# Weight sums of the couples: from GpSimd arithmetic to accumulating transfers, and result stores issued half a unit later

## The chip, the cores and the metric

The kernel runs on one core of one Trainium2 chip, as one program. The time is the device time of one execution in microseconds; the number that counts is the median of several executions. Engine names as in the profile: PE is TensorE, PEld its weight loads, DVE is VectorE, ACT is ScalarE, POOL is GpSimd, SP is SyncE. Three of them also issue transfers: SP, ACT and POOL.

## The reference, cut to what matters

The reference is one layer of a hybrid decoder over a prompt of 2048 tokens of width 1024, plus 8 single-token samples, all in float32:

```python
hn = rmsnorm(x) * (1 + scale) + shift
xa, za, q, k, v, glr, zg = split(hn @ w_in)        # widths 1024, 1024, 512, 512, 1024, 16, 1024
xc = conv4(xa); gx, ga = sigmoid(block_diag(xc))   # RG-LRU group
log_a = 8 * ga * log_sigmoid(lru_lambda); a = exp(log_a)
u = sqrt(1 - exp(2 * log_a)) * gx * xc
h_t = a_t * h_{t-1} + u_t
y_lru = h * silu(za)
o = gated_linear_attention(q, k, v, glr)           # 4 heads, per-head RMSNorm
y_gla = o * silu(zg)
x = x + gate * (concat(y_lru, y_gla) @ w_out); y = rmsnorm(x) * g_final
```

The change concerns the columns xa, za and zg of the input projection, and the products with SiLU that follow them.

## The kernel before, in words

The prompt is worked off in two halves of 1024 tokens (TH). In each half the four GLA heads come first (`gla_head`), then the *couples*: pairs of 128-column blocks of `w_in`. `Lru(half, j)` couples columns XA+128j and ZA+128j; `Zg(half, h)` couples the two blocks of zg of one head. A half has eleven couples. The output projection (class `Pair`) follows after the second half.

A couple is a product of weights (1024 by 256) with activations (1024 by 1024), each seen as a 2 by 2 matrix of blocks. It is computed with a scheme of Strassen's kind (Winograd's form): seven block products instead of eight. The right-hand operands are A11, A12, A21, A22 and four combinations S1 to S4, made once per half and kept in SBUF; the weights are B11, B12, B21, B22 and the combinations T1 to T4. Every operand is held as a high part (fp32r) and a low rest, so one product is 4 x 3 matmuls of 128 x 512, into PSUM (`Couple.product`, line 1558). Between products, sums of PSUM banks are made on DVE and ACT (lines 1562 to 1573), and the four results of a couple go to `block`, which applies the convolution and gates (Lru) or the SiLU and the product with the attention output (Zg), and stores them with `spill` (line 712) into the DRAM tensor `mixd`. In the first half the couples' stores are issued by ACT's queue, in the second half by POOL's.

In the first half the weights come raw: `load_raw` fetches 1 MB into one of two buffers, and `prepare(q)` splits one operand with `split`: ACT copies the high part (line 1504), DVE subtracts it for the low part (line 1505), and SP stores both for the second half (line 1507). The combinations are made inside the raw buffer: after B11 is split, `combine` overwrites b11 with T1, makes T2 in a tile `t2`, and overwrites b12 with T3 (lines 1538 to 1540), and after T1 is split, b11 becomes T4 (line 1522). POOL makes these sums, except for the first couple, where DVE makes three of them. `combine` also runs small TensorE products for the samples (line 304, `sample_cols`), which read the raw weights before they are overwritten; their result leaves through the copy in line 305 and the products in line 310. In the second half the split operands are simply read back (`src`).

The order of work is written by hand: `couples` lists the uses of the operands, interleaving two neighbouring couples, and calls `prepare` five uses ahead (`lead=5`). Each use advances a clock by half a unit (`tick(0.5)`), and `after(units, f)` emits `f` when the clock has got that far. Within an engine, instructions run in the order that the framework's scheduler gives them; `behind(q)` ties an emission to the last instruction of queue q.

Of the kernel before, what the change touches and what calls it, by code (L numbers as in the profile page):

```python
# [53 lines left out]
def hybrid_kernel(ctx, tc, i, o):  # L54
# [654 lines left out]
    def spill(y, ct, half, c0, q=S):  # L709

        t0 = (half * TH + c0) // P
        q.dma_start(mixd[t0:t0 + 4, :, ct].rearrange("t p c -> p t c"), y.rearrange("p (t c) -> p t c", c=P))

    def behind(q):

        return tc.issue_after(next(x for x in reversed(list(nc.cur_bb.bb.instructions)) if x.engine == q.engine))
# [403 lines left out]

    def silu(z, src):
        log_exp[0] = False
        S.activation(z, src, AF.Tanh, scale=0.5)
        V.scalar_tensor_tensor(z, z, 1.0, src, op0=OP.add, op1=OP.mult)

# [187 lines left out]
    def second_rows(sc, ready, then):  # L1313
# [22 lines left out]
        def step(p, x, k):  # L1336
            if p == 0 and not ready:
                after(0.5, lambda: step(p, x, k))
                return
            pt = turn(x, (k, k + 4))  # L1340
            f = sc.tile([P, 4, P], F32, tag="f", bufs=2)
            for m in range(2):
                S.activation(f[:, 2 * m:2 * m + 2], pt[:, m * 256:(m + 1) * 256].rearrange("p (j t) -> p j t", j=2),
                             AF.Identity, scale=Gm[:, k + 4 * m, 8:9], bias=Sh[:, k + 4 * m, 8:9])
            G.dma_start(fd[0:4, :, k, p * P:(p + 1) * P].rearrange("o p c -> p o c"), f)
            b = sc.tile([P, 4, P], F32, tag="s", bufs=2)
            G.tensor_tensor(b[:, 0], f[:, 1], f[:, 3], op=OP.add)
            G.tensor_tensor(b[:, 1], b[:, 0], f[:, 0], op=OP.subtract)
            G.tensor_tensor(b[:, 2], f[:, 0], f[:, 1], op=OP.subtract)
            G.tensor_tensor(b[:, 3], f[:, 2], b[:, 1], op=OP.subtract)  # L1350
            G.dma_start(fd[4:8, :, k, p * P:(p + 1) * P].rearrange("o p c -> p o c"), b)
            if k < 3:
                after(1 if k == 1 else 0.5, lambda: step(p, x, k + 1))
            elif p < 3:
                load(p + 1)
            else:
                after(1.5, then)
# [6 lines left out]
    def sums(pool, then):  # L1364
# [8 lines left out]
        def one(k):  # L1373
            s1, s2 = two()
            (h11, l11), (h21, l21), (h22, l22) = [high_low(op, k) for op in (A11, A21, A22)]
            with behind(V):
                add(s1, h21, h22)
                add(s1, s1, l21)

            def more():  # L1380
                with behind(V):
                    add(s1, s1, l22)
                    add(s2, s1, h11, OP.subtract)
                    add(s2, s2, l11, OP.subtract)
                after(0.5, high)
# [15 lines left out]
        def other(k, s2, low):  # L1401
            s3, s4 = two()
            (h11, l11), (h21, l21), (h12, l12) = [high_low(op, k) for op in (A11, A21, A12)]
            with behind(V):
                add(s4, h12, s2, OP.subtract)
                add(s4, s4, l12)

# [56 lines left out]
    class Couple:  # L1464
# [30 lines left out]
        def prepare(self, q, now=False):  # L1495
# [13 lines left out]
            if q == B11:  # L1509
                self.slot(q)  # L1510
                split(q, b11)
                (lambda: self.combine(V)) () if now else after(self.wait, self.combine)
            elif q == T2:
                self.slot(q)
                if now:
                    split(q, self.t2)
                else:
                    after(0.5, lambda: split(q, self.t2))
            elif q == T1:
                self.slot(q)  # L1520
                split(q, b11)
                G.tensor_tensor(b11, b21, self.t2, op=OP.subtract)
            else:
                self.slot(q)
                split(q, {B21: b21, T3: b12, B22: b22, T4: b11}[q])

        def combine(self, q=G):
            r = self.raw
# [8 lines left out]
            t = self.t2 = lp.tile([P, 4, P], F32, tag="t2", name="t2")  # L1537
            q.tensor_tensor(b11, b12, b11, op=OP.subtract)
            q.tensor_tensor(t, b22, b11, op=OP.subtract)
            q.tensor_tensor(b12, b22, b12, op=OP.subtract)  # L1540

# [5 lines left out]
        def product(self, q):  # L1547
# [15 lines left out]
            elif q == 1:  # L1563
                V.tensor_tensor(self.y, self.y, self.p1, op=OP.add)
            elif q == 2:
# [22 lines left out]
    class Zg(Couple):  # L1588
# [34 lines left out]
        def block(self, s, dt, src):  # L1623
            z = self.zs()
            silu(z, src)
            c0 = SEGS[s][0]
            V.tensor_tensor(z, z, self.o[((0, 0), (1, 1), (0, 1), (1, 0)).index((s, dt))], op=OP.mult)
            spill(z, 8 + 2 * self.h + dt, self.half, c0, G if self.half else S)

    smp_lru = {}  # L1630

    class Lru(Couple):
# [18 lines left out]
        def block(self, s, n, src):  # L1651
            if n == 1:
                z = self.zs()
                silu(z, src)
                after(2, lambda: self.out(s, z))
            else:
                self.conv(s, src)
                after((2.5, 2)[s], lambda: self.gates(s))
# [57 lines left out]
        def out(self, s, z):  # L1716
            if not self.res:
                after(0.5, lambda: self.out(s, z))
                return
            c0 = SEGS[s][0]  # L1720
            V.scalar_tensor_tensor(z, self.res[0][:, c0:c0 + 512], 0.5, z, op0=OP.mult, op1=OP.mult)
            spill(z, self.j, self.half, c0, G if self.half else S)

# [761 lines left out]
```

## Time and profile before

| | |
|---|---|
| median of 3 executions | 1461.93 us (1461.71 to 1464.23) |
| profiled execution: its time, its span | 1465.7 us, 1463.9 us |
| PE busy in the span | 1417.0 us (97%) |
| DVE, ACT, POOL busy | 1096.9, 697.1, 205.3 us |
| mean granted TensorE clock | 0.988 |
| first half's couples | about 332 to 600 us |
| second half's couples | about 880 to 1128 us |

The profiled execution is a separate one; its time is 3.8 us above the median. PE's busy time is modelled, since matmuls are pipelined. In rows of instructions the columns are line, engine, operation, output and inputs, count, busy us and mean ns of one, then the engine's idle time just before and what ended it. In rows of waits the engine that waits stands left of the arrow, then total us, number and longest.

### The profile page before, as it was taken

The numbers are of one execution on the slowest core, as the hardware profiler recorded it, in microseconds if no ns is written. First come the engines' busy times: TensorE is split into PE (matmuls) and PEld (weight loads), VectorE is DVE, ScalarE is ACT, GpSimd is POOL, SyncE is SP. The second block draws the span as 40 slices with busy tenths as digits, with TensorE's granted clock in tenths as the row PEclk, the third lists the DMA queues.
The fourth block names the chain that finished last, engine by engine and source line by source line (L and its number), as shares of the span: only waits on it lengthen the run. The fifth ranks groups of instructions, "written<-read, shape, count | busy, mean of one in ns | idle before, by whom it ended". The sixth has DMA issues, their size and how long they took to land.

```text
span 1463.9 us, 22541 instructions
## 1 busy us (share of the span) xinstructions
PE 1417.0 (97%) x8113; PEld 1172.2 (80%) x8113; DVE 1096.9 (75%) x2405; ACT 697.1 (48%) x1310; POOL 205.3 (14%) x255
## 2 busy tenths in 40 slices
PE   8999999999999999999999999998999999999997
PEld 6888989886777777889888888887788787777786
DVE  5767975657888788766776865797966886688886
ACT  4634463635674767334343533766563522144332
POOL 0200154425222212001111100000002000000000
PEclk9999999999999999999999999999999999999999
DMA  9725666648668557965857528888889867684452
GB/s 325 266 88 167 244 229 209 233 134 283 236 242 280 201 195 273 354 218 174 313 170 238 189 87 302 283 278 269 280 258 385 317 228 271 230 339 144 135 173 101
DMA packets 173380, 341.89 MB, mean 234 GB/s; under 512 B 12466, under 2 KB 101842, under 8 KB 169677
## 3 DMA queue, kind: packets, MB, share of 16 engines
q1 hardware_dynamic: 137269, 277.92, 55.7%
q0 software_dynamic: 13392, 46.54, 8.2%
q10 hardware_dynamic: 22608, 15.99, 3.4%
q8 instruction: 64, 1.05, 0.3%
q14 instruction: 47, 0.39, 0.1%
HBM read 205.78 MB, written 134.69 MB: 233 GB/s over the span
## 4 chain that ended last, share of the span: by engine, by line
PE 64%; DVE 12%; DMA 8%; ACT 7%; issue 6%; POOL 1%; SPq 1%; ACTq 0%; DVEq 0%; POOLq 0%
PE acc L2132 11%; PE tp L2132 8%; PE acc L1558 8%; PE tp L1558 7%; PE acc L397 3%; PE acc L396 3%; PE acc L398 3%; PE acc L702 3%; PE acc L704 3%; PE acc L703 3%; DVE cv L1676 2%; DVE tg L1712 2%; PE po L1048 1%; DMA wada<-in_w_ada_dram 1%; DMA op<-fd 1%
## 5 line engine op out<-in xcount | busy, mean ns | idle before, releaser
L1558 PE MATMUL acc<-op,op 128*128 128x512 f32 x1056 | 252.2, 393 | 3.1 <-ACT op L1504 2.8
L1558 PEld LDWEIGHTS acc<-op,op 128*128 128x128 f32 x1056 | 198.5, 189 | 45.9 <-ACT op L1504 3.3
L1558 PE MATMUL tp<-op,op 128*128 128x512 f32 x792 | 201.1, 401 | 2.4 <-DVE acc L1568 2.4
L2132 PE MATMUL acc<-w,a 128*128 128x512 f32 (+1 forms) x792 | 189.3, 392 | 2.8 <-DVE w L1997 2.0
L1558 PEld LDWEIGHTS tp<-op,op 128*128 128x128 f32 x792 | 150.7, 193 | 36.4 <-DVE acc L1568 3.4
L2132 PEld LDWEIGHTS acc<-w,a 128*128 128x128 f32 x792 | 147.9, 189 | 39.8 <-issue 3.4
L396 PE MATMUL acc<-w,op 128*128 128x256 f32 (+1 forms) x508 | 150.4, 296 | 1.5 <-ACT w L374 1.2
L397 PE MATMUL acc<-w,op 128*128 128x256 f32 (+1 forms) x508 | 144.2, 284 | 0.4 <-DVE w L375 0.4
L398 PE MATMUL acc<-w,op 128*128 128x256 f32 (+1 forms) x508 | 144.0, 283 | 0.2 <-DVE op L271 0.2
L2132 PE MATMUL tp<-w,a 128*128 128x512 f32 x564 | 137.2, 393 | 0.0
L2132 PEld LDWEIGHTS tp<-w,a 128*128 128x128 f32 x564 | 105.2, 188 | 27.9 <-issue 5.2
L702 PE MATMUL acc<-op,w 128*128 128x512 f32 x296 | 121.2, 410 | 0.0
L704 PE MATMUL acc<-op,w 128*128 128x512 f32 x296 | 116.7, 394 | 0.0
L703 PE MATMUL acc<-op,w 128*128 128x512 f32 x296 | 115.9, 392 | 0.0
L396 PEld LDWEIGHTS acc<-w,op 128*128 128x128 f32 x508 | 96.2, 190 | 3.3 <-ACT w L374 1.6
L397 PEld LDWEIGHTS acc<-w,op 128*128 128x128 f32 x508 | 95.6, 188 | 1.6 <-DVE w L375 0.6
L398 PEld LDWEIGHTS acc<-w,op 128*128 128x128 f32 x508 | 95.7, 188 | 0.6 <-DVE op L271 0.4
L1994 ACT CAST a<-s 128x512 fp32r<-128x512 f32 x61 | 36.5, 619 | 104.3 <-issue 37.2
L228 ACT ACTIVATE junk<-on 128x256 bf16<-128x256 f32 x64 | 26.8, 418 | 111.3 <-DVE on L1053 98.8
L1676 DVE SCALAR_TENSOR_TENSOR cv<-xa,vecT,cv 128x512 f32<-128x512 f32 x96 | 73.0, 760 | 7.5 <-ACT cv L1674 6.7
L1049 DVE TENSOR_TENSOR states<-states,pkv 128x256 f32<-128x256 f32 x60 | 25.1, 418 | 54.6 <-PE po L1048 54.3
L704 PEld LDWEIGHTS acc<-op,w 128*128 128x128 f32 x296 | 55.6, 188 | 12.5 <-DVE w L375 0.4
(445 smaller groups left out, 2818.8 us busy)
## 6 DMA issues: line engine op xcount, KB each, us to landing
wtd<-op SPq DMA_DIRECT2D x77, 512.0 KB
op<-wtd SPq DMA_DIRECT2D x77, 512.0 KB
w<-parts SPq DMA_DIRECT2D x16, 1024.0 KB
a<-mixd SPq DMA_DIRECT2D x63, 256.0 KB
parts<-w POOLq DMA_DIRECT2D x12, 1024.0 KB, 6.5
w<-wd SPq DMA_DIRECT2D x10, 1024.0 KB
wr<-in_w_in_dram SPq DMA_DIRECT2D x18, 512.0 KB
wada<-in_w_ada_dram SPq DMA_DIRECT2D x16, 512.0 KB
```

Source lines behind the costliest of these rows:

```text
L228: S.activation(junk[:m, :n], x, AF.Square, accum_out=out)
L396: PE.matmul(ps, part(0, kt, c), hi[:, kt % 4], start=kt == 0, stop=False)
L397: PE.matmul(ps, part(0, kt, c), lo[:, kt % 4], start=False, stop=False)
L398: PE.matmul(ps, part(1, kt, c), hi[:, kt % 4], start=False, stop=kt == KT - 1)
L702: PE.matmul(ps[:, :n], hi[:, kt], a, start=kt == 0, stop=False)
L703: PE.matmul(ps[:, :n], hi[:, kt], b, start=False, stop=False)
L704: PE.matmul(ps[:, :n], lo[:, kt], a, start=False, stop=kt == KT - 1)
L1558: PE.matmul(ps, w[:, u, k], t[:, v, k], start=q < 3 and (k, u, v) == (0, 0, 0), stop=(k, u) == (3, 1), skip_group_check=True)
L1676: V.scalar_tensor_tensor(cv, xa[:, k:k + 512], cw[k], cv, op0=OP.mult, op1=OP.add)
L1712: V.tensor_tensor_scan(h, a, tx, 0.0 if self.half == 0 else hc[:, j:j + 1], op0=OP.mult, op1=OP.add)
L1994: S.copy(t[:, 0, k], (low(t) if src is None else src)[:, k])
L2132: PE.matmul(ps, t[:, u, k], w[:, v, k, c], start=(q < 3 or ps is own) and (k, u, v) == (0, 0, 0), stop=(k, u) == (3, 1), skip_group_check= ...
```

## The change

Four things change.

1. Signs. S1, S2, S4 and the corresponding operands of the second half (in `second_rows`) change sign, so that the weights' combinations become plain sums: T1 = b11 + b12, T2 = b22 + T1, T3 = b12 + b22, T4 = b21 + T2. Where a result then comes out negated, `silu` takes -1 for its constant, and one sum of PSUM banks becomes a difference.
2. Place of the sums. For all couples but the first, POOL's four operations go; ACT copies b22 into `t2`, and four transfers issued by POOL with an accumulating operation add in place: b11 += b12, t2 += b11, b12 += b22 and, when B21 has been split, b21 += t2. T4 is then split from b21 instead of b11.
3. T2 is split a whole unit after `prepare` instead of half a unit.
4. `late_spill`: in the first half the couples' stores are emitted half a unit later, behind ACT's last instruction at that time. In the second half nothing changes (POOL).

```diff
+    def late_spill(z, ct, half, c0):
+        def go():
+            with behind(S):
+                spill(z, ct, half, c0)
+        if half:
+            spill(z, ct, half, c0, G)
+        else:
+            after(0.5, go)
...
-    def silu(z, src):
+    def silu(z, src, sign=1.0):
...
-        V.scalar_tensor_tensor(z, z, 1.0, src, op0=OP.add, op1=OP.mult)
+        V.scalar_tensor_tensor(z, z, sign, src, op0=OP.add, op1=OP.mult)
...
             if q == B11:
                 self.slot(q)
                 split(q, b11)
-                (lambda: self.combine(V)) () if now else after(self.wait, self.combine)
+                self.now = now
+                (self.combine if now else lambda: after(self.wait, self.combine))()
...
-                    after(0.5, lambda: split(q, self.t2))
-            elif q == T1:
-                self.slot(q)
-                split(q, b11)
-                G.tensor_tensor(b11, b21, self.t2, op=OP.subtract)
+                    after(1, lambda: split(q, self.t2))
             else:
                 self.slot(q)
-                split(q, {B21: b21, T3: b12, B22: b22, T4: b11}[q])
+                split(q, {T1: b11, B21: b21, T3: b12, B22: b22, T4: b21}[q])
+                if q == B21:
+                    self.add(b21, b21, self.t2)
+
+        def add(self, out, x, y):
+            if self.now:
+                V.tensor_tensor(out, x, y, op=OP.add)
+            else:
+                G.dma_start(out, y, accum_op=OP.add)
...
-            q.tensor_tensor(b11, b12, b11, op=OP.subtract)
-            q.tensor_tensor(t, b22, b11, op=OP.subtract)
-            q.tensor_tensor(b12, b22, b12, op=OP.subtract)
+            if not self.now:
+                S.copy(t, b22)
+            self.add(b11, b11, b12)
+            self.add(t, b22 if self.now else t, b11)
+            self.add(b12, b12, b22)
...
-                V.tensor_tensor(self.y, self.y, self.p1, op=OP.add)
+                V.tensor_tensor(self.y, self.p1, self.y, op=OP.subtract)
...
-            silu(z, src)
+            silu(z, src, -1.0 if dt else 1.0)
...
-            spill(z, 8 + 2 * self.h + dt, self.half, c0, G if self.half else S)
+            late_spill(z, 8 + 2 * self.h + dt, self.half, c0)
...
-            spill(z, self.j, self.half, c0, G if self.half else S)
+            late_spill(z, self.j, self.half, c0)
```

The sums that make S1, S2, S4 (in `sums`) and those in `second_rows` only swap additions and subtractions, one for one.

More of the change, by code (lines that the diff above doesn't have):

```diff
@@ L1346, in step @@
             b = sc.tile([P, 4, P], F32, tag="s", bufs=2)
-            G.tensor_tensor(b[:, 0], f[:, 1], f[:, 3], op=OP.add)
-            G.tensor_tensor(b[:, 1], b[:, 0], f[:, 0], op=OP.subtract)
+            G.tensor_tensor(b[:, 0], f[:, 3], f[:, 1], op=OP.subtract)
+            G.tensor_tensor(b[:, 1], b[:, 0], f[:, 0], op=OP.add)
             G.tensor_tensor(b[:, 2], f[:, 0], f[:, 1], op=OP.subtract)
-            G.tensor_tensor(b[:, 3], f[:, 2], b[:, 1], op=OP.subtract)
+            G.tensor_tensor(b[:, 3], b[:, 1], f[:, 2], op=OP.subtract)
             G.dma_start(fd[4:8, :, k, p * P:(p + 1) * P].rearrange("o p c -> p o c"), b)
@@ L1376, in one @@
             with behind(V):
-                add(s1, h21, h22)
-                add(s1, s1, l21)
+                add(s1, h22, h21, OP.subtract)
+                add(s1, s1, l21, OP.subtract)
             def more():
@@ L1382, in more @@
                     add(s1, s1, l22)
-                    add(s2, s1, h11, OP.subtract)
-                    add(s2, s2, l11, OP.subtract)
+                    add(s2, s1, h11)
+                    add(s2, s2, l11)
                 after(0.5, high)
@@ L1404, in other @@
             with behind(V):
-                add(s4, h12, s2, OP.subtract)
-                add(s4, s4, l12)
+                add(s4, s2, h12, OP.subtract)
+                add(s4, s4, l12, OP.subtract)
             def last():
@@ L1517, in prepare, with combine @@
                 else:
-                    after(0.5, lambda: split(q, self.t2))
-            elif q == T1:
-                self.slot(q)
-                split(q, b11)
-                G.tensor_tensor(b11, b21, self.t2, op=OP.subtract)
+                    after(1, lambda: split(q, self.t2))
             else:
                 self.slot(q)
-                split(q, {B21: b21, T3: b12, B22: b22, T4: b11}[q])
-        def combine(self, q=G):
+                split(q, {T1: b11, B21: b21, T3: b12, B22: b22, T4: b21}[q])
[5 more added lines that the diff above has]
+            else:
+                assert out is x
+                G.dma_start(out, y, accum_op=OP.add)
+        def combine(self):
             r = self.raw
@@ L1653, in block @@
                 z = self.zs()
-                silu(z, src)
+                silu(z, src, -1.0)
                 after(2, lambda: self.out(s, z))
```

## The prediction

> **What bounds the kernel now.** I read the page's head first, then the table of busy time by stage, then, for the one stage that the change works in, the waits of TensorE, and from each of them the timeline backwards.
>
> ```profile
> span 1463.9 us, 22541 instructions
> ...
> PE 1417.0 (97%) x8113; PEld 1172.2 (80%) x8113; DVE 1096.9 (75%) x2405; ACT 697.1 (48%) x1310; POOL 205.3 (14%) x255
> ```
>
> TensorE is busy in 97% of the span, so the whole kernel cannot gain more than what TensorE idles or loses in clock. The couples of the first half, the only place where sums are made from raw weights, lie from about 332 to 600 us (columns: stretch, length, busy us and instructions of PE, weight load, DVE, ACT, POOL, granted clock, DMA share, GB/s):
>
> ```profile
> 332.00:600.00 268.00, 256.14 (x1208) 200.48 (x1209) 222.19 (x321) 175.95 (x274) 71.43 (x50) 0.97 0.71 248
> ```
>
> TensorE idles 11.9 us of 268, and the clock of 0.97 says that it loses some more. DVE is busy 83%, ACT 66%: neither bounds on average, but they fall behind in bursts. Who ends TensorE's idle time there (waited for, us in total, times, longest):
>
> ```profile
> PE acc L310 <- ACT am L305: 3.9, 2, 2.2
> PE acc L1558 <- ACT op L1504: 2.8, 1, 2.8
> PE gps L1693 <- ACT xh L1680: 2.6, 2, 1.7
> PE tp L1558 <- DVE acc L1568: 2.4, 1, 2.4
> PE acc L304 <- DVE tp L1564: 1.2, 1, 1.2
> PE acc L1558 <- DVE zs L1124: 0.3, 1, 0.3
> ```
>
> 13.2 us in seven holes: this list is the purse from which any gain in the stage is paid. The 2.8 us is the start of the stage (the first split), which the change leaves alone.
>
> **Part 1: the sums leave POOL.** For ten couples three POOL sums (L1538 to L1540) and the later difference for T4 (L1522) go; in the first couple DVE does them, with one more add of 0.7 us that T4 needs only six products later (taken at 0, at most 0.7).
>
> ```profile
> L1505 DVE TENSOR_TENSOR op<-raw,op 128x512 fp32r<-128x512 f32 x66 | 54.6, 836 | 5.9 <-ACT op L1504 5.8
> ...
> L1681 DVE TENSOR_TENSOR xl<-cv,xh 128x512 fp32r<-128x512 f32 x16 | 10.9, 684 | 0.1
> ```
>
> The same DVE operation on the same shape takes 684 ns in L1681 and 836 in L1505, the line whose instructions meet POOL's sums: 66 x 0.152 = 10.0 us of DVE time that comes back. A single victim shows the size:
>
> ```profile
> 525.87 1.78 DVE L1505 TENSOR_TENSOR op<-raw,op 128x512 fp32r<-128x512 f32 x1
> ```
>
> 1.78 instead of 0.68 is 1.1 us, and the chain of waits hands it on: the cv operation after it releases ACT's xh, behind which ACT works without a hole through exponential, Tanh, Sqrt and table loads to the gate's product on DVE, and DVE from there through the scan and the next cv to a hole of TensorE twenty us later:
>
> ```profile
> 547.85 0.50 PE L1693 MATMUL gps<-xh,amh 128*128 128x512 f32 x1 [1.66 <-ACT xh L1680]
> ```
>
> So of the two L1693 holes (2.6 us: 1.7 and 0.9) I take 1.1 off the longer and all 0.9 of the shorter: 2.0 us. The hole of 1.2 us behind L1564 goes whole (DVE backlog of the same kind), and half of the 2.4 behind L1568, which ends a DVE queue of scan, products and a split: 1.2.
>
> A shortened hole also saves clock. In the ten us around the hole at 547.85 the granted clock is 0.83:
>
> ```profile
> 545.00:555.00 10.00, 8.34 (x29) 6.13 (x28) 9.96 (x16) 7.19 (x12) 1.63 (x1) 0.83 0.84 265
> ```
>
> That is 1.7 us lost on top of the hole. If the hole falls from 1.66 to 0.6 us, I take that the loss goes with it: 1.7. The Trainium skill ("TensorE: Matmul & The Clock Gate", Part 1: The HAM clock gate) says that the clock is halved after an idle window of about 3.4 us. By that rule a hole of 1.66 us would cost no clock, and my sum would be 1.7 us smaller; the trace does not agree with it as worded, since the clock fell here with no idle of 3.4 us, so I keep the row.
>
> **Part 2: stores wait half a unit.** In the first half each result store sits in ACT's queue directly behind the DVE product it sends out, so ACT stands until DVE is done:
>
> ```profile
> 440.64 0.62 ACT L1504 CAST op<-t 128x512 fp32r<-128x512 f32 x1 [3.42 <-POOL t L1539]
> ...
> 445.73 1.61 ACTq L712 DMA_DIRECT2D mixd<-zs  x3
> ...
> 447.38 0.37 ACT L305 COPY am<-acc 128x256 f32<-128x256 f32 x1 [4.68 <-DVE zs L1627]
> ...
> 447.80 0.30 PEld L310 LDWEIGHTS acc<-sel,am 128*128 128x128 f32 x2 [2.19 <-ACT am L305]
> ```
>
> Read upwards: TensorE waits for the small copy am; that copy waits 4.68 us on ACT behind three stores, which wait for DVE. With the stores emitted half a unit (one product of TensorE) later, the copy passes: of the 3.9 us in two L310 holes this one, 1.7 us, goes, and the 0.3 behind L1124 just before it. The other L310 hole (2.2) stays: no store stands before it. The same store also holds the gate activation of the next segment:
>
> ```profile
> ACT tx L1697 <- DVE tg L1712: 12.4, 5, 3.4
> ...
> ACT tg L1697 <- DVE zs L1721: 6.8, 4, 1.7
> ...
> ACT zs L1123 <- DMA mixd<-zs: 4.1, 1, 4.1
> ```
>
> The 6.8 us of ACT go too, at nothing for TensorE, since its consumer xh hangs on DVE. What is late next: zs has four buffers, and one store's landing already held ACT for 4.1 us; a product later in issue lengthens that one wait. And at the end of the stage the chain runs over a store into the next stage's weights:
>
> ```profile
> 592.80 5.47 DMA mixd<-zs
> 598.29 7.58 DMA w<-parts
> ```
> ```profile
> 605.98 0.19 PEld L396 LDWEIGHTS acc<-w,op 128*128 128x128 f32 x1 [0.42 <-issue]
> ```
>
> The weights land at 605.87, and TensorE's weight load, idle for 0.42 us, follows at once, so nothing covers a later store there: one product, by the following row 2.7 us, is charged in full.
>
> ```profile
> 883.42 2.75 PE acc L1558 x12
> ```
>
> **Part 3: what the accumulating transfers cost.** Added are ten copies of b22 into t on ACT and forty 256 KB transfers issued on POOL, which has no other work in these couples. The copy is like L1504's cast (0.62 us below): 6.2 us of ACT in 268, set against 6.8 us of stores' waits that leave it; 0 on the path. The issue takes 0.75 us of POOL:
>
> ```profile
> L712 POOL DMA_DIRECT2D mixd<-zs x27 | 20.2, 752 | 270.4 <-DVE zs L1721 231.4 <-DVE zs L1627 29.6 <-issue 7.8
> ```
>
> No accumulating transfer is in the trace. The nearest rows are plain POOL transfers of 256 KB, of this stage and of the second half's couples, where DMA is busier (last column: us from issue to landing):
>
> ```profile
> fd<-scratch POOLq DMA_DIRECT2D x3, 256.0 KB, 2.8
> ```
> ```profile
> mixd<-zs POOLq DMA_DIRECT2D x25, 256.0 KB, 5.4
> ```
>
> What hangs on it is T2. Its operand t needs two transfers one after the other, where POOL did two sums:
>
> ```profile
> ACT op L1504 <- POOL t L1539: 15.4, 6, 4.8
> ```
> ```profile
> 460.70 1.28 POOL L1538 TENSOR_TENSOR raw<-raw 128x512 f32<-128x512 f32 x1 [5.65 <-PE acc L304]
> ```
> ```profile
> 463.38 0.62 ACT L1504 CAST op<-t 128x512 fp32r<-128x512 f32 x1 [1.87 <-POOL t L1539]
> ```
>
> Of the ten T2s six hold ACT, 15.4 us in all, 4.8 at most. In the couple shown, before: t is there 2.7 us after POOL starts, ACT arrives at 0.8 and waits 1.9. After: t is there at 2 x (0.75 + 2.8) = 7.1 us or 2 x (0.75 + 5.4) = 12.3, and ACT arrives one product later, at 0.8 + 2.7 = 3.5: a wait of 3.6 or 8.8 us. I take the 2.8 of the same stage: 3.6 us is the size of the present waits on t (3.42 above), and ACT has idle time right after (12.4 us in 5 waits for the scan) that it eats first. TensorE needs T2 five products later. So 0 on the path, and the rival below has the other end. The Trainium skill ("DMA: Bandwidth & Descriptors", Anatomy of one DMA — SWDGE (gpsimd) path) fits such a transfer as 2.0 us plus bytes over 436 GB/s, an estimate of 2.6 us here; by it the wait would be 3.2 and the sum the same. The row of 2.8 agrees with it, the row of 5.4 does not.
>
> Sign changes in T1, S1, S2, S4 and the SiLUs replace one operation by another of the same shape: 0. Where b21 takes its sum, T4 is split five products later: 0. The second half's stores were on POOL and stay.
>
> **Sum.** Holes: 1.7 + 0.3 + 2.0 + 1.2 + 1.2 = 6.4. Clock: 1.7. End of stage: -2.7. Net 5.4 us. The profiled execution (span 1463.9, its time 1465.7) would come to 1460.3; its time lies 3.8 above the median 1461.93, so the median goes to 1456.5. Own range of this case: without clock and with 0.7 for the first couple 1459.0, without the charge at the end 1453.8. A difference under 0.2% (2.9 us) is about what a measurement of this kernel cannot tell from none.
>
> **Rivals.**
>
> A, slower: T2's chain takes over. If a transfer lands after 5.4 us, ACT waits 8.8 us where it waited up to 4.8. In the burst of 437 to 448 us ACT stood 3.4 + 4.7 us and TensorE lost 2.0. At that rate six couples lose 6 x 2.0, three of them clock of 1.7 as well, and the end is charged: 12 + 5.1 + 2.7 = 20 us; the gains of part 1 (about 4 of holes) and part 2 (2.0) still come, so +14: 1476. It decides when a transfer lands after more than about 3.4 us (a wait above 4.8). For it: accumulating reads the destination as well. Against: POOL's queue is free, and TensorE's holes stood beside only one of six present waits on t.
>
> B, slower: DMA becomes the limit.
>
> ```profile
> q10 hardware_dynamic: 13200, 6.56, 8.2%
> ```
>
> This queue (ACT's stores, same 512-byte pieces) uses 8.2% of 268 us, 22 us, for 6.56 MB. Forty times 0.262 MB are 10.5 MB: 35 us, or 70 if the destination's reading costs as much. On 0.71 x 268 = 190 that is 225 to 260 us of 268. At the upper end the present wait on raw weights grows and loads come late in every couple:
>
> ```profile
> ACT op L1504 <- DMA raw<-in_w_in_dram: 3.4, 5, 1.3
> ```
>
> The stage then ends when DMA ends, about 274 us with the first uncovered loads, +6: 1468.
>
> C, hidden: DVE's and ACT's time comes back, but the holes stay where they are, because another operation in the same queues is late; only the end and a hole or two move: 1461.
>
> D, more: all holes but the first go, 10.4 us, with three losses of clock of 1.7, and the end is covered because all of its chain comes earlier: 15.5, so 1446.5.
>
> **How the numbers follow.** Forecast 0.43, A 0.18, B 0.11, C 0.18, D 0.10. Faster by over 0.2%: forecast and D, 0.53; within: C, 0.18; slower: A and B, 0.29. The likeliest is 1456.5; the range from 1449 to 1473 leaves out most of D and half of A.
>
> **What would show it.** L1505's mean falls from 836 to about 690 ns (part 1). No ACT wait on L1627 or L1721 remains before L305 and L1697, and the hole at L310 of 1.7 us is gone (part 2). ACT's wait on t is now on a transfer, in total near 15 to 25 us; above 40 it is A. Landing of the accumulates near 3 us, above 3.4 points to A; the stage's DMA share at 0.84 or less, above 0.93 it is B. The weights of the next stage come up to 2.7 us late at its start; if TensorE does not wait there, that charge was wrong.

## The result, and the profile after

The changed kernel is slower. Its median is 1534.16 us (1529.45 to 1537.92), the kernel before 1463.08 us in the same comparison: a ratio of 1.0456 [1.0427, 1.0485], some 71 us, where the prediction had 1456.5 with a range of 1449 to 1473. The profiled execution took 1537.92 us. The head of its page:

```profile
span 1536.2 us, 22600 instructions
...
PE 1435.9 (93%) x8113; PEld 1185.6 (77%) x8113; DVE 1079.1 (70%) x2406; ACT 701.5 (46%) x1320; POOL 192.0 (12%) x254
```

TensorE works on the same 8113 matmuls, but for 93% of the span instead of 97%. The table of busy time by stage, first over the window in which the couples lay before, then over the one that they take now (columns: stretch, length, busy us and instructions of PE, weight load, DVE, ACT, POOL, granted clock, DMA share, GB/s):

```profile
332.00:600.00 268.00, 222.52 (x1017) 172.57 (x1016) 162.25 (x263) 143.64 (x230) 52.42 (x47) 0.90 0.84 229
332.00:668.00 336.00, 275.35 (x1236) 214.18 (x1235) 207.95 (x328) 181.35 (x286) 60.70 (x54) 0.89 0.84 237
```

In the old window TensorE does 1017 instructions where it did 1208. From the couples' first product to the first matmul of the next stage it took 333.36 to 603.72 us before and takes 337.65 to 669.02 now: 61.0 of the 72.3 us of span. (4.3 us lie ahead of the stage, in which the first 100 us had a clock of 0.91 in this execution, 0.97 before; 7.0 are scattered behind it.) The waits of TensorE in the stage:

```profile
PE gps L1712 <- ACT xh L1699: 25.9, 5, 10.1
PE tp L1577 <- DVE acc L1587: 12.7, 2, 9.0
PE acc L310 <- ACT am L305: 11.0, 4, 6.9
PE tp L1577 <- ACT op L1515: 7.3, 1, 7.3
PE acc L1577 <- ACT op L1515: 3.6, 1, 3.6
```

Together 60.5 us, where the purse before held 13.2: 47 us of new holes, four of the five rows behind ACT. The rest of the 61 is busy time: the same matmuls take 274.4 us instead of 259.9, at a granted clock of 0.89 instead of 0.97. And what ACT waits for in the same stretch:

```profile
ACT op L1515 <- DMA t<-raw: 45.4, 5, 13.8
ACT t L1556 <- DMA raw<-t: 22.7, 6, 6.4
ACT op L1515 <- issue: 14.7, 2, 12.0
```

The first row is the split of T2, waiting for t += b11. The second is a wait that the prediction does not have: the copy of b22 into t stands until the *previous* couple's b21 += t has finished reading t, since t has one buffer. The third row, which names no releaser, is the first wait again: both of its splits of t start 0.07 us after a transfer into t has landed, so ACT stands some 60 us for T2's sum. The transfers themselves (POOL's queue in this stretch: packets, MB, share of the 16 DMA engines; then the issues, last column: median us from issue to landing):

```profile
q0 software_dynamic: 21600, 12.06, 26.5%
...
raw<-raw POOLq DMA_DIRECT2D x20, 256.0 KB, 4.8
...
t<-raw POOLq DMA_DIRECT2D x10, 256.0 KB, 4.7
raw<-t POOLq DMA_DIRECT2D x10, 256.0 KB, 7.0
```

The chain of waits shows how they stand in a row. Two couples meet here (start, duration, what):

```profile
466.47 12.27 DMA raw<-t
...
478.76 0.03 ACT t L1556
...
480.17 0.53 ACT op L1515
480.70 2.90 issue
483.61 9.32 DMA t<-raw
...
492.95 0.03 ACT op L1515
...
493.47 0.60 ACT zs L1134
...
494.70 0.70 DVE acc L1587
...
495.45 5.02 PE tp L1577 x12
```

One couple's b21 += t lands 12.3 us after its issue; only then ACT copies b22 into t, and POOL sums into it; that lands 9.3 us later; only then ACT splits T2, and everything queued behind that split on ACT (stores, a SiLU) runs, which DVE needs for the bank sum that TensorE stood for. (The chain goes on with ACT's queue 0.03 us after the copy and the split have started; each of them runs for 0.62 us.) On POOL, which issues all forty, the same couple's sums are these (start, duration, then its idle time before):

```profile
466.47 1.29 POOL L1542 DMA_DIRECT2D raw<-t  x1 [12.05 <-ACT tg L1716]
479.05 1.30 POOL L1542 DMA_DIRECT2D raw<-raw  x1 [11.29 <-DMA raw<-t]
483.61 1.29 POOL L1542 DMA_DIRECT2D t<-raw  x1 [3.26 <-issue]
493.24 1.30 POOL L1542 DMA_DIRECT2D raw<-raw  x1 [8.34 <-DMA t<-raw]
```

Each of the last three starts 0.31 to 0.64 us after the landing of the one before. The first and the tenth T1 start at 346.80 and 616.13 us, 29.9 us a couple; before, POOL's sums for T1 (L1538) started at 342.07 and 557.45 us, 23.9 a couple. The queue alone explains much of that. From issue to landing the forty transfers take 248 us of the 303 between the first issue and the last landing, and no two are in flight together: four of them in a row are 24.8 us, more than a couple took before.

### The profile page after: what moved, and what is told of

It is laid out like the page before. It is cut to its first block, busy times and chain, and to the rows that moved or that the text cites. A ratio compares the mean times of both kernels' runs of the same rounds, so it can differ in the third digit from the quotient of the medians.

```text
span 1536.2 us, 22600 instructions
## 1 busy us (share of the span) xinstructions
PE 1435.9 (93%) x8113; PEld 1185.6 (77%) x8113; DVE 1079.1 (70%) x2406; ACT 701.5 (46%) x1320; POOL 192.0 (12%) x254
## 4 chain that ended last, share of the span: by engine, by line
PE 45%; DMA 9%; DVE 8%; ACT 4%; issue 4%; SPq 1%; POOL 0%; ACTq 0%; DVEq 0%; POOLq 0%
PE acc L2151 11%; PE tp L2151 8%; PE tp L1577 5%; PE acc L1577 5%; DMA raw<-t 2%; PE acc L702 2%; PE acc L704 2%; PE acc L703 2%; PE acc L396 1%; PE acc L397 1%; PE acc L398 1%; DVE tg L1731 1%; DMA op<-fd 1%; DMA mixd<-zs 1%; DMA t<-raw 1%
## 5 line engine op out<-in xcount | busy, mean ns | idle before, releaser
L1577 PE MATMUL tp<-op,op 128*128 128x512 f32 x792 | 209.6, 413 | 20.3 <-DVE acc L1587 12.7
L1577 PEld LDWEIGHTS tp<-op,op 128*128 128x128 f32 x792 | 156.6, 201 | 57.5 <-DVE acc L1587 14.0
L396 PEld LDWEIGHTS acc<-w,op 128*128 128x128 f32 x508 | 96.9, 191 | 2.9 <-ACT w L374 1.6
L1135 DVE SCALAR_TENSOR_TENSOR zs<-zs,acc 128x512 f32<-128x512 f32 x49 | 33.4, 684 | 45.3 <-ACT zs L1134 44.3
```

Of the source, the lines that this page charges most:

```text
L396: PE.matmul(ps, part(0, kt, c), hi[:, kt % 4], start=kt == 0, stop=False)
L1135: V.scalar_tensor_tensor(z, z, sign, src, op0=OP.add, op1=OP.mult)
L1577: PE.matmul(ps, w[:, u, k], t[:, v, k], start=q < 3 and (k, u, v) == (0, 0, 0), stop=(k, u) == (3, 1), skip_group_check=True)
```

## The experiments

Three theories stood at the start. **W**: ACT works in order and stands for tile t (the landing of T2's sum, and t's release). **L**: the accumulating transfers load the DMA engines, so that everything else lands late. **S**: the late stores. Each kernel has a ratio to the kernel before with its 95% interval; the diffs are against the changed kernel unless something else is said.

### Which part of the change

**late_only**: the kernel before with `late_spill` alone.

```diff
-            spill(z, self.j, self.half, c0, G if self.half else S)
+            late_spill(z, self.j, self.half, c0)     # and in Zg
```

> The kernel before with the late stores alone (sums on POOL, signs as before). Theory W (ACT, in order, stands for the tile t, whose two sums are now two slow transfers and whose buffer the previous couple's transfer still reads): the stores are innocent, 1456 to 1466 us. Theory L (the accumulating transfers load the DMA engines): the same. Theory S (the later stores hold the four zs buffers and the next stage's weights): 1490 us or more, with waits of ACT L1123 on DMA mixd<-zs far above 4 us.

Measured: 1.0014 [0.9994, 1.0035]. The late stores are worth nothing that shows in the time. ACT's waits show why:

```profile
ACT tg L1708 <- DVE zs L1732: 6.8, 4, 1.7
...
ACT am L305 <- DVE op L1516: 5.3, 1, 5.3
```

The 6.8 us are where they were, and the 4.7 us before the copy in line 305 became 5.3. Neither wait hung on the store's place alone. The copy overwrites am, and a DVE product reads am just before; in the kernel before:

```profile
446.22 0.68 DVE L1627 TENSOR_TENSOR zs<-zs,am 128x512 f32<-128x512 f32 x1
```

In late_only the same product runs from 447.18 to 447.86 us, four stores still stand in ACT's queue between 446.69 and 448.93, and the copy starts at 448.97. In the same way the gate's activation overwrites tg, which the product zs<-tg,zs (L1721) reads.

**accum_early**: the changed kernel with the stores at their old place.

```diff
-            after(0.5, go)
+            spill(z, ct, half, c0)
```

> The changed kernel with the stores issued as early as before; signs, accumulating transfers and the T2 delay stay. W and L: still 1525 to 1545 us, a little above the changed kernel since ACT waits in two places. S: back to 1470 us or less.

Measured: 1.0437 [1.0381, 1.0493], as slow as with late stores. S is out.

**pool_sums**: signs, late stores and T2's place as changed, but the sums by POOL arithmetic and no copy on ACT.

```diff
-                G.dma_start(out, y, accum_op=OP.add)
+                G.tensor_tensor(out, x, y, op=OP.add)
```

> The changed kernel with its four sums per couple done by POOL arithmetic again (t made directly from b22 and b11, so ACT's copy goes too); signs, late stores, T2's delay of a whole unit and the place of T4's sum stay. W and L: 1455 to 1468 us, everything comes back. S: still above 1490 us. It also tells what the signs, the stores and T2's delay are worth together against before: W expects a gain of 0 to 6 us.

Measured: 1.0000 [0.9975, 1.0025]. So signs, late stores and the later T2 together make no difference that can be told, and the whole loss is in turning POOL's sums into transfers.

**dve_sums**: the same with all sums on DVE.

```diff
-                G.dma_start(out, y, accum_op=OP.add)
+            V.tensor_tensor(out, x, y, op=OP.add)
```

> The changed kernel with all four sums of every couple on DVE: neither POOL nor transfers. It adds 40 x 0.7 = 28 us to DVE in the stage and takes away what POOL's arithmetic costs it (some 15 us), so 1462 to 1475 us. It is the base for the next run.

Measured: 0.9957 [0.9941, 0.9974], faster than before, and just under the range that was expected, although DVE took up 28 us of sums. The prediction's reading of line 1505 was right: without POOL's sums beside it that instruction is fast (here L1516 on raw, the same in the changed kernel):

```profile
L1516 DVE TENSOR_TENSOR op<-raw,op 128x512 fp32r<-128x512 f32 x66 | 45.0, 691 | 4.4 <-ACT op L1515 4.4
```

691 ns instead of 836; where POOL still does the sums it is 772 (pool_sums) and 867 (late_only). **dve_early** is this kernel with the stores at their old place (the edit of accum_early).

> All sums on DVE, signs changed, T2 a unit later, but the stores of the first half issued where the kernel before has them. It asks whether the later stores are worth anything beside DVE's sums. S (the later stores are worth nothing, as the kernel with these alone showed at 1.0014) expects 0.993 to 0.998, the same as with the later stores (0.9957); if they help, 0.998 to 1.002.

Measured: 0.9971 [0.9952, 0.9991]: the intervals overlap, and again nothing hangs on the stores.

### What it is about the transfers

**plain_dma**: the same transfers, overwriting instead of accumulating, so the sums are left out.

```diff
-                G.dma_start(out, y, accum_op=OP.add)
+                G.dma_start(out, y)
```

> The changed kernel with plain transfers in place of the accumulating ones: same bytes, same 512-byte pieces, same order and waits, but the sums are left out (the destination is overwritten). If the accumulating is what is dear: packets on POOL's queue fall from 67 ns to about 27 ns, the landing from about 5 to 3 us, POOL's issue from 1.29 to 0.75 us, and the time to 1475 to 1500 us under W (two transfers in series are still 7 us), to below 1475 under L (the DMA share falls by about 0.15). If the time stays above 1520, it is neither the size nor the accumulating but the waits' order alone.

Measured: 1.0064 [1.0040, 1.0088]. The order, the number and the bytes of the transfers are the same, and six sevenths of the loss are gone (0.6% is left of 4.6). Its 1475.92 us lies at the edge between W's range and L's and does not decide between them. POOL's queue, and POOL's timeline over one couple:

```profile
q0 software_dynamic: 3613, 11.82, 11.6%
```
```profile
445.98 0.76 POOL L1542 DMA_DIRECT2D raw<-raw  x1 [7.10 <-DVE tp L1583]
450.47 0.75 POOL L1542 DMA_DIRECT2D t<-raw  x1 [3.73 <-ACT op L1515]
451.21 0.75 POOL L1542 DMA_DIRECT2D raw<-raw  x1
```

A plain transfer takes POOL 0.75 us instead of 1.29, and T3's follows T2's at once, at 451.21; with accumulation the same two were 9.63 us apart (483.61 and 493.24). The plain queue moved nearly the same bytes in packets of 3.3 KB and used 11.6% of 280 us, 32 us; accumulating, in packets of 558 bytes, 26.5% of 343 us, 91 us: 2.8 times as much.

**accum_2k**: the raw tile laid out block by block, so that a sum's pieces are 2 KB long instead of 512 bytes; still accumulating. (Zg's weights then come in two loads of 512 KB, as Lru's do anyway.)

```diff
-  b11, b12, b21, b22 = [r[:, 4 * k:4 * k + 4, b] for k ...]    # raw: [P, KT, 2, P]
+  b11, b12, b21, b22 = [r[:, b, 4 * k:4 * k + 4] for k ...]    # raw: [P, 2, KT, P]
```

> The changed kernel with the raw weights laid out by block, so that one row of a block is one piece of 2 KB instead of four of 512 bytes; everything else, all 40 accumulating transfers and all waits, as changed (the two gated-attention couples that loaded 1 KB rows now load 512-byte rows, as the others do). If the price goes by pieces (67 ns for each of 512 bytes): POOL's packets fall to a quarter or a third, the queue's share from 26% to below 15%, landing in bursts to 5 us, time 1465 to 1490 us. If it goes by bytes: 1520 to 1540 us.

Measured: 1.0179 [1.0151, 1.0206]. Over half of the loss comes back, so the size of the pieces carries much of the price, though less than "by pieces" expected: 1495.91 us lies between the two ranges, and the queue's share fell to 20.1% and not below 15%. POOL's timeline has the reason beside the bytes' time: T3's transfer is issued 0.54 us after T2's, where with short pieces it came 4.2 us later or more.

```profile
461.17 0.88 POOL L1539 DMA_DIRECT2D t<-raw  x1 [5.29 <-DMA raw<-raw]
461.71 1.23 POOL L1539 DMA_DIRECT2D raw<-raw  x1
```

So accumulating transfers can overlap; those in 512-byte pieces did not. The row T1, T2, T4 is still there, and 1.8% is left.

**urgent_pool**: T1 and T2 by POOL arithmetic again, T3 and T4 by transfers.

```diff
-            self.add(b11, b11, b12)
-            self.add(t, b22 if self.now else t, b11)
+            e = V if self.now else G
+            e.tensor_tensor(b11, b11, b12, op=OP.add)
+            e.tensor_tensor(t, b22, b11, op=OP.add)
```

> The changed kernel with the two sums that T2 waits for (b11 + b12, then t) as POOL arithmetic, without ACT's copy; the other two (b12 and b21) stay accumulating transfers, 20 instead of 40. No ACT instruction needs a transfer's result soon. W (ACT's waits for t): 1460 to 1475 us, nearly everything comes back. L (load on the DMA engines): half of the load stays, so about half of the 60 us: 1490 to 1505 us.

Measured: 1.0052 [1.0034, 1.0070], at the same DMA share of 0.85 in 332 to 600 us as the changed kernel's 0.84. What is left of the loss probably stands on POOL, where the sums now queue behind transfers: ACT waited 29.0 us for POOL's t, 7.9 at most.

**pool_copy** and **pool_copy_later**: the copy of b22 on POOL instead of ACT; then T2 split a further unit later as well.

```diff
-                S.copy(t, b22)
+                G.tensor_copy(t, b22)
...
-                    after(1, lambda: split(q, self.t2))
+                    after(2, lambda: split(q, self.t2))      # pool_copy_later only
```

> The changed kernel with one edit: POOL, not ACT, copies b22 into t. All forty accumulating transfers stay, and ACT still waits for T2. ACT's wait for the earlier couple's b21 += t (22.7 us in the changed kernel) moves to POOL. W expects that about a third of the loss comes back, 1.02 to 1.037; L expects no change, 1.043 to 1.048. If it comes out slower than the changed kernel, the copy on POOL makes T2 later still.

Measured: 1.0417 [1.0383, 1.0450], above W's range.

> As the kernel with POOL's copy, and T2 is split two units after its place in the order instead of one, so that the two transfers in a row have about two products (5.4 us) more. All forty accumulating transfers stay. W expects that ACT's wait on t falls from 45 us to under 15 and most of the loss comes back: 1.005 to 1.02. L expects 1.04 to 1.048. A third way: T2's low part comes so late that TensorE waits for it at its product (holes behind ACT op and DVE op at TensorE's couple line), then 1.03 to 1.05 with small ACT waits on t.

Measured: 1.0391 [1.0366, 1.0417]. W as worded failed here: with one ACT wait taken away and a unit more of room for the other, a seventh of the loss came back. In pool_copy_later:

```profile
ACT op L1515 <- DMA t<-raw: 47.5, 5, 11.9
POOL t L1542 <- DMA raw<-raw: 45.6, 9, 11.9
POOL t L1556 <- DMA raw<-t: 42.5, 5, 11.6
```

ACT waits for t as long as before (45.4), because t is later too. A fixed delay would have been covered by the unit; a *ring* isn't. So W was widened. **Chain**: a couple's sums stand in one row on POOL, T1, T2, T3, T4, the next couple's t needs the T4 before it, T4 needs B21's split, and that is behind T2's split on ACT. The row's length sets the couple's period, and no shift of one step inside it helps much.

### Load by itself

These kernels take dve_sums (0.9957), so no sum is a transfer, and add accumulating transfers that nobody should need. In three of the four a wait of their own came in, so their totals don't answer the question.

**dve_load**: 38 transfers into the idle tile gls.

```diff
             self.add(b12, b12, b22)                  # dve_sums
+            for k in range(n_of_couple):             # 3 or 5, together 38
+                G.dma_start(gls_half(k % 2), ident4, accum_op=OP.add)
```

> dve_sums with 38 accumulating transfers of 256 KB in 512-byte pieces on POOL that nothing waits for (a constant added into a tile that is free there): the DMA load of the change without its waits. L: 40 to 60 us above dve_sums. W: at most 10 us above it, though the DMA share rises to the changed kernel's 0.84.

Measured: 1.0300 [1.0273, 1.0326]. By its total that is L, but the tile was not idle to the end: the transfers came late, and a load of the Zg couples into gls waited 36.2 us for them. One stretch before that is clean: from 445 to 560 us 15 accumulating transfers into SBUF follow each other without a pause. First dve_load, then dve_sums:

```profile
445.00:560.00 115.00, 113.92 (x561) 90.08 (x561) 99.70 (x163) 79.19 (x123) 19.34 (x15) 1.00 0.95 267
```
```profile
445.00:560.00 115.00, 114.02 (x564) 90.78 (x563) 101.97 (x170) 83.02 (x130) 0.00 (x0) 1.00 0.68 239
```

TensorE's busy time is the same to 0.1 us at a DMA share of 0.95; in the changed kernel it is 96.9 us in this stretch.

**dram_load**: forty into a DRAM tensor of their own, from a constant tile.

```diff
+            load(self, 0); load(self, 1); load(self, 2)     # dve_sums, in combine; load(self, 3) behind B21
+    def load(c, n): G.dma_start(sink[n], ident4, accum_op=OP.add)     # plain in the first couple
```

> All sums on DVE (as in the kernel that came out at 0.9957), and in each of the ten later couples of the first half four accumulating transfers of 256 KB in 512-byte pieces issued by POOL at the places of the changed kernel, into a DRAM tensor that nothing reads; four plain ones fill it in the first couple. No engine but POOL waits for any of them. L (the load on the DMA engines delays everything else) expects most of the loss: 1.025 to 1.045, about 1500 to 1530. W (what costs is that ACT stands for the accumulated tiles) expects 0.995 to 1.006, 1460 to 1475, although the DMA share of 332 to 600 us rises to about 0.84 as in the changed kernel.

Measured: 1.1178 [1.1147, 1.1209], which no theory expected. With no operand of the couples in them, the scheduler issued all forty at the start, from 12.0 to 221.7 us, and they held up POOL's own work there: TensorE stood 119.7 us for POOL's rows of line 269. About the couples it says nothing. But it shows forty transfers in a row: 5.4 us each, with 4.3 us to land.

**dram_load2**: the same, from the split operands T1, T2, T3 and B21, which ties them to their couples.

```diff
                 S.copy(w[:, 0], x)                           # dve_sums, in split
+                if q in (T1, T2, T3, B21): load(self, n, w[:, 0])
```

> All sums on DVE (0.9957 by itself). Beside them, in each of the ten later couples of the first half, four accumulating transfers of 256 KB in 512-byte pieces on POOL's queue, from the split operands T1, T2, T3 and B21 into a DRAM tensor that nothing reads: as many bytes and pieces as the changed kernel's, at about the same times, and nobody waits for them but the reuse of an operand's slot. Load expects 1.02 to 1.045, 1495 to 1530. Chain expects 0.994 to 1.006, 1457 to 1475, with a granted clock of 0.97 or more in 340 to 560 us at a DMA share of 0.82 or more.

Measured: 1.0284 [1.0257, 1.0311]. Again a wait had come in: POOL fell behind, and the reuse of an operand's slot waited for a transfer that still read it.

```profile
ACT op L1516 <- DMA sink<-op: 30.2, 8, 9.7
```

**ident_load**: a constant tile added to the stored operands in DRAM, each behind its store; no tile in SBUF is released by it.

```diff
                 SP.dma_start(self.keep[q], w.bitcast(F32))   # dve_sums
+                if q in (T1, T2, T3, B21) and self.m:        # not in the first couple
+                    G.dma_start(self.keep[q][:, 0], ident4, accum_op=OP.add)
```

> All sums on DVE (0.9957 by itself), and forty accumulating transfers of 256 KB in 512-byte pieces on POOL, four to each of the ten later couples: a constant tile is added to the stored operands T1, T2, T3 and B21 in DRAM, each behind its store. The first half reads none of these, and no tile in SBUF is written or released by them; the second half's operands are changed by it, so its output is not the reference's. Load expects 1.02 to 1.045, 1495 to 1530, with a clock under 0.96 in 340 to 560 us. Chain expects 0.995 to 1.008, 1460 to 1478, with 0.97 or more there at a DMA share of 0.82 or more. Both expect that two of these transfers are never issued less than 4 us apart, as in the changed kernel.

Measured: 1.0112 [1.0085, 1.0140], over chain's 1.008 and under load's 1.02. The stage settles it, 340 to 560 us, first of dve_sums, then of ident_load, then of the changed kernel:

```profile
340.00:560.00 220.00, 218.74 (x1078) 174.14 (x1077) 193.47 (x320) 152.65 (x239) 0.00 (x0) 1.00 0.72 252
```
```profile
340.00:560.00 220.00, 214.42 (x1054) 169.22 (x1053) 189.81 (x311) 149.13 (x234) 32.44 (x25) 1.00 0.98 276
```
```profile
340.00:560.00 220.00, 178.27 (x794) 138.32 (x793) 125.91 (x206) 113.04 (x179) 38.20 (x31) 0.88 0.83 226
```

With the DMA engines busy 98% of the time and 25 accumulating transfers issued (28 in the changed kernel, whose POOL column counts three other instructions too), TensorE lost 4.3 us of 220 and no clock. The changed kernel, at 83%, lost 40.5 us against dve_sums. What ident_load loses in total, 1.55% over dve_sums or 23 us, comes mostly later: POOL's backlog lasted until 675 us, a memset on POOL stood behind it, and TensorE waited 11.0 us for what hung on that:

```profile
PE pkv L1053 <- DVE kTl L1035: 11.0, 1, 11.0
```

Its timeline on POOL is the cleanest look at the transfers one after another:

```profile
652.26 1.29 POOL L1523 DMA_DIRECT2D wtd<-ident  x1 [6.16 <-issue]
656.80 1.30 POOL L1523 DMA_DIRECT2D wtd<-ident  x1 [3.25 <-issue]
664.97 1.29 POOL L1523 DMA_DIRECT2D wtd<-ident  x1 [6.87 <-issue]
```

None of these uses the result of another. They were never less than 4.5 us apart, 8.0 on the average (40 from 363.94 to 674.69; in the changed kernel never less than 4.2), with landings of 4.2 to 13.2 us, 6.6 in the median. Each of the 39 that follow was issued 0.31 us after the one before it had landed.

### Which of the four sums

All against dve_sums, with the sums named as accumulating transfers and the others on DVE; `add` takes the name of the sum. Where T2 is a transfer, ACT's copy of b22 stays, issued behind T1's sum instead of ahead of it.

```diff
-            V.tensor_tensor(out, x, y, op=OP.add)
+            if self.now or n not in by_transfer:
+                V.tensor_tensor(out, x, y, op=OP.add)
+            else:
+                G.dma_start(out, y, accum_op=OP.add)
```

**t3_only**: T3.

> T1, T2 and T4 on DVE, only T3 (b12 += b22) as a transfer: 10 transfers, needed several products later. Chain expects them free, 0.993 to 0.999, at or under the 0.9957 of all sums on DVE, since DVE has 7 us less to do. Load expects a quarter of the changed kernel's loss on top of 0.9957: 1.004 to 1.01.

Measured: 0.9943 [0.9924, 0.9961], the fastest of all kernels here (1459.59 us), though not told apart from dve_sums. Ten transfers that are needed only several products later cost nothing that shows, and they landed after 5.6 us in the median.

**t4_only**: T4.

> T1, T2 and T3 on DVE, only T4 (b21 += t) as a transfer: 10 transfers, and the next couple's t waits for each. Chain expects little, because one landing of 7 to 9 us fits between the split of B21 and the next couple's sums: 0.995 to 1.004. Load expects 1.004 to 1.01, the same as T3 alone.

Measured: 1.0073 [1.0047, 1.0098], above what chain expected and inside load's range, though load had expected the same of T3 alone. The landings, 10.7 us in the median instead of 7 to 9, did not fit: DVE, writing the next t, waited for it, and ACT for DVE.

```profile
DVE t L1539 <- DMA raw<-t: 21.0, 3, 7.2
...
ACT op L1515 <- DVE t L1539: 13.7, 5, 7.4
```

**t12_only**: T1 and T2.

> T3 and T4 on DVE, T1 and T2 as transfers one behind the other, with ACT's copy of b22 into t: 20 transfers. Chain expects that this pair carries most of what is lost: 1.012 to 1.04, with ACT waiting 25 us or more for t. Load expects half of the loss, 1.012 to 1.025, and no more than the two others together (T3 alone and T4 alone).

Measured: 1.0154 [1.0132, 1.0176], in both ranges; but it is more than T3 alone and T4 alone lose together over dve_sums (1.1%), which load excluded, and ACT's wait for t is what chain expected:

```profile
ACT op L1515 <- DMA t<-raw: 37.8, 8, 8.4
```

**t4_dve**: T1, T2 and T3.

> T4 (b21 += t) on DVE, the other three sums by thirty accumulating transfers. Chain expects the loss of T1 and T2 (1.0154) and a little more, because T3's transfer stands in POOL's queue between T2's and the next couple's T1 without being waited for: 1.014 to 1.025. Load expects three quarters of the changed kernel's loss, 1.03 to 1.038.

Measured: 1.0214 [1.0180, 1.0248], in chain's range and not in load's.

Over dve_sums, in per cent of the time: T3 -0.1, T4 1.2, T1 with T2 2.0, the three first 2.6, all four 5.0. Transfers of equal bytes and pieces have very unequal prices, by where they stand. The parts one by one make 3.0; the other 2.0 come only when all four stand on POOL, T4 behind T3 behind T2 and the next t behind T4.

So the cause is shown as far as this: the loss is in the accumulating transfers, it depends on which of them are waited for, and the load on the DMA engines without such a wait cost 4.3 us in 220 (ident_load) and 0.1 in 115 (dve_load). Not separated are two reasons why all four cost more than their parts: the queue, which four transfers one after the other fill by themselves (24.8 us a couple), and t's one buffer, which ties the next couple to T4's landing. Why accumulating transfers in 512-byte pieces never overlap on POOL's queue, and those in 2 KB pieces do, the traces don't say. A second buffer for t, which would untie the couples with all forty kept, wasn't tried, since SBUF has no room for it; the full queue would remain.

## Why the prediction was wrong

**What bounds the kernel.** Right as far as it went: the purse was 13.2 us (in eight holes, not seven), and the change decided itself in this stage. What it lacked is the other side. A purse bounds the gain and not the loss, and the loss was worked out from ACT's waits at the old pace.

**Part 1, the sums leave POOL.** The first step held: L1505's 836 ns became 693 (the prediction: about 690). What it is worth in holes is only partly shown. The kernel without transfers, dve_sums, gained 6 us (0.43% of 1467.46), near the 6.1 that part 1 was given (2.0 + 1.2 + 1.2 of holes and 1.7 of clock), but that is luck as a check: it carries 28 us more of sums on DVE, and in its profile the holes behind xh are gone while the one behind DVE's bank sum grew from 2.4 to 7.3 us. No run shows the 1.7 of clock by itself.

**Part 2, the late stores.** Gain of 2.0 and charge of 2.7 were both wrong in their place. The time can't tell, since their difference of 0.7 us lies inside late_only's interval; the rows can. The prediction took "the copy passes" as the end of the wait. But the copy overwrites a tile that DVE's product reads, and stores still stood before it: in late_only TensorE's hole of 1.7 us at L310 is still there with 1.4. The 6.8 us on ACT, a wait of the same kind, did not go either. And TensorE did not wait for the next stage's weights, neither in late_only nor in the changed kernel, so the charge never came.

**Part 3, the transfers at 0 on the path.** This is the step that failed: it put the transfers at 0, and with POOL's arithmetic in their place (pool_sums) the whole loss is gone, 61 us of it in this stage. It went wrong in four places.

- *The landing.* Between the ends 2.8 and 5.4 us it took 2.8, "of the same stage", from plain transfers with three in the trace. Accumulating ones landed after 4.7 to 7.0 us in the median, by kind, and the plain ones of plain_dma after 3.3 to 6.6. By the page that the prediction names (the Trainium skill, "DMA: Bandwidth & Descriptors", Anatomy of one DMA) it would be an estimate of 2.6 us; none of these medians agrees with that.
- *The issue.* 0.75 us was the plain one; an accumulating one takes POOL 1.29 us, and POOL's next one came 4.2 us later or more, T3's 9.6 us after T2's above. "POOL has no other work in these couples" was true and beside the point: its queue was the row.
- *t's release.* The copy of b22 into t was priced by its duration, 6.2 us, and not by what it waits for. In `combine` the tile is asked for anew, with one buffer, whose last reader is the earlier couple's b21 += t, now a transfer of 7 us and no longer a POOL sum of 1.7 (L1522, both in the median). That wait was 22.7 us on ACT.
- *The cover.* "TensorE needs T2 five products later" was no cover, because ACT stands meanwhile for everything else. TensorE's largest row, 25.9 us, is a gate's xh behind ACT, not T2; for T2 itself it stood once, 7.3 us.

**Rival A** named the right mechanism and the right test (a landing over 3.4 us, ACT's wait on t over 40; it was 45.4), and gave it 0.18 and 1476. Its price was a fifth of the truth (+14 of 71), since it counted six couples at 2.0 us of holes and a fixed wait each. In a ring the wait of one couple is the start of the next: the period went from 23.9 to 29.9 us, and over the nine periods between the first and the tenth T1 that is 54 of the 61 us that the stage lost.

**Rival B** (DMA the limit, 225 to 260 of 268 us) was wrong as the cause. Its load was too small, not too large: POOL's queue took 91 us of the DMA engines, where 35 or 70 were expected, and the share of 0.84 held for a stage a quarter longer. But ident_load at 0.98 shows that this much load by itself takes 4 us.

**Rivals C and D**, a gain that stays hidden and a larger one, did not come as priced, but C's mechanism, another wait in place of the one taken away, is what late_only shows.

The signs at 0 and T4's split from b21 at 0 were right by pool_sums.

## What to carry to other kernels

When arithmetic in place is turned into a transfer, list who waits for the landing, who may not overwrite its source until then, and which queue issues the next; if these close a ring from one turn of the loop to the next, the ring's length is the loop's period, and moving one step in it is worth little (here a seventh of the loss at most). Count the issuing queue too: if its transfers land one after the other, their landings add up to a period of their own. An accumulating transfer is no plain one: take its price from a run, with the pieces that it will have, and give it only to sums that nobody needs soon (here T3 alone was free, and all four cost 5% over DVE's sums). A load test must be free of waits of its own, and its verdict is read from the stage and not from the total: the totals of three of four here measured something else.

## What the hardware showed that was not expected

- Accumulating transfers of 256 KB in 512-byte pieces never overlapped on POOL's queue, in the changed kernel or in the load tests: 4.2 us apart or more, each issued 0.31 us or more after the landing of the one before. Plain ones are issued 0.75 us apart, accumulating ones in 2 KB pieces 0.54.
- The same bytes in accumulating form took 2.8 times the time of the DMA engines (91 against 32 us for 12 MB), in packets of 558 bytes instead of 3.3 KB.
- TensorE hardly felt DMA engines that were busy 98% of 220 us: 4.3 us and a clock of 1.00.
- Holes came with a lower clock: with 47 us more of them the granted clock was 0.89 over 336 us, against 0.97 in the stage before.
